# Output projection of a hybrid encoder block: buffers, banks and the order of its pools rearranged

## Chip, core and metric

The kernel runs on one core of a Trainium2 chip. The metric is the device time of one execution in microseconds (us). A difference is called faster or slower from 0.3% on.

## What is computed

One block of a streaming encoder on 2048 tokens of width 1024, in float32. The reference, cut to what matters:

```
xn   = rms_norm(x, norm1_gain);  proj = xn @ w_in
ret  = silu(gate) * head_norm(retention(rotary(q), rotary(k), v))     # 4 heads of 128
rw   = rwkv7_time_mix(proj[..., 2048:], ...)                          # 8 heads of 64, a recurrence in time
h    = x + concat([ret, rw]) @ w_out                                  # the output projection
h    = h + hier_moe(rms_norm(h, norm2_gain), ...)                     # 32 experts, 2 for each token
out  = rms_norm(h, final_norm_gain)
```

## The kernel before

**Two phases with memory of their own.** SBUF and PSUM are given out in pools that are stacked from two ends, "left" (low addresses) and "right" (high addresses), in the order in which they are opened. Within a pool the tiles lie in the order in which the code first takes them, each with its number of buffers. Phase one closes its pools (`rw` left, `ga` right) ahead of the opening of those of phase two, so a tile of phase two lies on bytes or banks of phase one. Its first writer waits until the last reader of each tile that lay there is done (`reuse_waits="tile"`). A planner that runs at build time fixes the order of each engine's instructions and of SyncE's DMA queue: of what is ready in its model it takes the highest priority, and `tc.high_priority(offset=...)` raises one.

**Phase one** walks over four groups of 512 tokens (`g`). The combined projection makes transposed features with matmuls into the two `pj` banks. The RWKV features go through DRAM (`pf_d`) to units of 128 tokens (`u`, 16 of them): `rwkv_prep` loads a unit's features, among them the gate features `lg` (L400, three buffers), and ends with masked products `pt`; a triangular solve runs on GpSimd (L486, L488); `rwkv_inv` completes the inverse on TensorE (from L511 on); `rwkv_chain` carries the state through two chunks; `rwkv_fin` normalizes the rows, multiplies them by the gate that it makes from `lg` with matmuls into `psi` (the line before L579), and writes them to `mx_d` (L580). After the last group's projections the RWKV of the last units is still running. Retention runs once for each head and group in `core`, from the bank `pk`; the last one of all, (g, h) = (3, 3), takes the `pj` banks. It ends with a product of the normalized rows and the head's gate `gs` (L651) and a write to `mx_d` (L652).

**The left side of phase one** opens with the pool `tr`. Its first tile is `lg` (128 columns, 512 bytes a partition, three buffers), then eight buffers of 2048 bytes named `tr`. The left PSUM banks are `pb` (two), `psr`, `psi` and `psz`. The right side opens with `gc` (retention's constants, state and values), then `xp` (x0 to x7), `ntp` (nT0 to nT7), `wh`, `wr`, `ev`, `rk` (kT, qT, gs) and `rc`; its banks are `pj` (two) and `pk`.

**Phase two** first makes the output projection. Its weights are split into a high and a low half (L168, L169) as `wo0` to `wo7`, from raw tiles of two buffers (`mraw`). `tile2(t)` does so with a tile of 128 tokens, whose mixed features are read back from `mx_d` into the same two raw buffers (L737) and split into `mT`. Then 48 matmuls of 512 columns fill two accumulators `acc` (k from 7 down to 0; for each k three matmuls for each half of the columns), and VectorE adds them to the tile's x (L754), which was loaded to `hx` (L742). For tiles 0 to 7 `hx` lies in the pool `hxp` (named `w4`, three buffers), from 8 on in `rwp` (named `raw`, eight buffers). `post(tiles)` routes them: TensorE transposes `hx` with the identity in `ct` (L767), multiplies it by the router's weights, VectorE chooses groups and experts, GpSimd scatters the token numbers, and `hx`, scaled in place (L861), goes to `xt_d` (L862), after which its buffer is free. `ct`, the constant blob of 476 columns, is the first tile of the pool `k2` and is loaded by L698; its first reader is the copy at L710.

The pools of phase two before: left `rwp`, and the banks `tpp` (two) and `accl` (three); right `k2`, `s2`, `mrp`, `wop7`, `wop`, `hxp`, `xhp`, `mtp`, and three `accr` banks. Read with the right side of phase one, `k2` and `s2` lie on `gc` and x7, and `mT` on `rc`.

When all tiles are routed, the expert loop runs: 32 experts, whose weights stream through `rwp` and are split into `hlp`, with accumulators from `accr` and `accl`.

Of the kernel before, what the change touches and what calls it, by code (L numbers as in the profile page):

```python
# [9 lines left out]
F32 = mybir.dt.float32  # L10
F32R = mybir.dt.float32r
# [5 lines left out]
PSUM = bass.MemoryType.PSUM  # L17
# [6 lines left out]
NG = S // G  # L24
# [6 lines left out]
PRI, PRW, PRF, PRC, PRO = 2000, 10000, 9000, 10000, 0  # L31
# [5 lines left out]
NRAW, NSP = 8, ((4, 0, 0), (4, 0, 0), (4, 0, 0))  # L37
# [95 lines left out]
def build(tc, A, out, dbg=None, phases=3):  # L133
    nc = tc.nc
    V, SC, GP, PE, SY = nc.vector, nc.scalar, nc.gpsimd, nc.tensor, nc.sync
# [3 lines left out]
    mx_d = dram.tile([8, 128, S], F32, name="mx_d")  # L139
# [27 lines left out]
    def split_w(hl, raw):  # L167
        SC.copy(hl[:, 0], raw)  # L168
        V.tensor_tensor(hl[:, 1], raw, hl[:, 0].bitcast(F32), op=ALU.subtract)  # L169
# [11 lines left out]
    lp, gp = opener(rw, "left"), opener(ga, "right")  # L181
    tr, rp, sm, cp = lp("tr", 8), lp("rp", 1), lp("sm", 2), lp("cp", 1)
    pb, pr, py, pz = lp("pb", 2, space=PSUM), lp("pr", 1, space=PSUM), lp("py", 1, space=PSUM), lp("pz", 1, space=PSUM)
    gc, xp, ntp = gp("gc", 1), gp("xp", 1), gp("ntp", 1)
    wh, wr, ev, rk, rc = gp("wh", 3), gp("wr", 4), gp("ev", 3), gp("rk", 2), gp("rc", 4)
    pj, pkb = gp("pj", 2, space=PSUM), gp("pk", 1, space=PSUM)
    if True:
        cst = cp.tile([128, CST.shape[1]], F32, name="cst")
        SY.dma_start(cst, A["cst"])
# [421 lines left out]
            mk(f'ret{g}')  # L611

        def core(g, h, kT, qT, gs, vtm):
            pk = pj if (g, h) == (NG - 1, 3) else pkb
            pkn = "pj" if pk is pj else "pk"
            vs = slice((h % 2) * 128, (h % 2 + 1) * 128)
            pst = pk.tile([128, 4, 128], F32, name=pkn)
            for b in range(4):
                PE.transpose(pst[:, b], kT[:, b * 128:(b + 1) * 128], ident)
            ktm = rc.tile([128, 4, 128], F32, name="rc")  # L620
            SC.activation(ktm, pst, AF.Copy, scale=kdec[:, h:h + 1])
            pss = pk.tile([128, 4, 128], F32, name=pkn)
            for b in range(4):
                bs = slice(b * 128, (b + 1) * 128)
                mm(pss[:, b], kT[:, bs], qT[:, bs], b == 0, b == 3)
            sT = rc.tile([128, 4, 128], F32, name="rc")
            V.tensor_tensor(sT, pss, dmask[:, None, h * 128:(h + 1) * 128].to_broadcast([128, 4, 128]), op=ALU.mult)
            psk = pk.tile([128, 4, 128], F32, name=pkn)
            for b in range(4):
                mm(psk[:, b], ktm[:, b], vtm[:, b, vs], b == 0, b == 3)  # L630
            sb = rc.tile([128, 4, 128], F32, name="rc")
            V.tensor_copy(sb[:, 0], srt[:, h])
            for b in range(4):
                dst = sb[:, b + 1] if b < 3 else srt[:, h]
                V.scalar_tensor_tensor(dst, sb[:, b], G128[h], psk[:, b], op0=ALU.mult, op1=ALU.add)
            psy = pk.tile([128, 512], F32, name=pkn)
            for b in range(4):
                bs = slice(b * 128, (b + 1) * 128)
                mm(psy[:, bs], qT[:, bs], sb[:, b], b == 0, b == 3)
            y = rc.tile([128, 512], F32, name="rc")  # L640
            SC.activation(y, psy, AF.Copy, scale=qdec[:, h:h + 1])
            psy = pk.tile([128, 512], F32, name=pkn)
            for b in range(4):
                mm(psy[:, b * 128:(b + 1) * 128], sT[:, b], vtm[:, b, vs], b == 0, b == 3)
            V.tensor_tensor(y, y, psy, op=ALU.add)
            head_center(y, 4, 128, 1e-5, pk.tile([128, 512], F32, name=pkn))
            psn = pk.tile([128, 512], F32, name=pkn)
            for b in range(4):
                PE.transpose(psn[:, b * 128:(b + 1) * 128], y[:, b * 128:(b + 1) * 128], ident)
            mo = rc.tile([128, 512], F32, name="rc")  # L650
            V.scalar_tensor_tensor(mo, psn, hrg[:, h:h + 1], gs, op0=ALU.mult, op1=ALU.mult)  # L651
            SY.dma_start(mx_d[h, :, g * G:(g + 1) * G], mo)  # L652
# [37 lines left out]

    p2, wo_ = ExitStack(), ExitStack()
    lp, kp, gp = opener(p2, "left"), opener(p2, "right"), opener(wo_, "right")
    rwp, tpp, accl = lp("rwp", NRAW), lp("tpp", 2, space=PSUM), lp("accl", 3, space=PSUM)
    k2, s2, accr = kp("k2", 1), kp("s2", 2), kp("accr", 3, space=PSUM)
    mrp, wop7, wop, hxp, xhp, mtp = gp("mrp", 2), gp("wop7", 1), gp("wop", 1), gp("hxp", 3), gp("xhp", 2), gp("mtp", 2)
    if True:
        ct = k2.tile([128, CST2.shape[1]], F32, name="ct")
        SY.dma_start(ct, A["cst2"])  # L698
# [19 lines left out]
            for i in range(4):  # L718
                SY.dma_start(d.rearrange("(i p t) o -> i p (t o)", i=4, p=128)[i], fill[:, z])
        SY.dma_start(h_d[S:S + 128, :], A["x"][0:128, :])  # L720
        wo = [(wop7 if k == 7 else wop).tile([128, 2, 1024], F32R, name=f"wo{k}") for k in range(8)]
        for k in range(7, -1, -1):
            for hf in range(2):
                raw = mrp.tile([128, 512], F32, name="mraw")
                hs = slice(hf * 512, (hf + 1) * 512)
                SY.dma_start(raw, A["wout"][k][:, hs])
                split_w(wo[k][:, :, hs], raw)

        def w4(t):
            return rwp.tile([128, D], F32, name="raw") if t >= PRN else hxp.tile([128, D], F32, name="w4")  # L730
# [1 line left out]
        def tile2(t):  # L732
            r0 = t * 128
            mT = []
            for z in range(1, -1, -1):
                raw = mrp.tile([128, 512], F32, name="mraw").rearrange("p (k t) -> p k t", k=4)
                SY.dma_start(raw, mx_d[z * 4:z * 4 + 4, :, r0:r0 + 128].rearrange("k p t -> p k t"))  # L737
                m = mtp.tile([128, 2, 4, 128], F32R, name="mT")
                split_w(m, raw)
                mT.insert(0, m)  # L740
            hx = w4(t)
            SY.dma_start(hx, A["x"][r0:r0 + 128, :])  # L742
            ps = [accr.tile([128, 512], F32, name="acc") for _ in range(2)]
            for k in range(7, -1, -1):
                ma, mb = (mT[k // 4][:, z, k % 4] for z in range(2))
                for n in range(2):
                    ns = slice(n * 512, (n + 1) * 512)
                    mm(ps[n], ma, wo[k][:, 0, ns], k == 7, False)
                    mm(ps[n], mb, wo[k][:, 0, ns], False, False)
                    mm(ps[n], ma, wo[k][:, 1, ns], False, k == 0)  # L750
            for n in range(2):
                ns = slice(n * 512, (n + 1) * 512)
                with soon():
                    V.tensor_tensor(hx[:, ns], ps[n], hx[:, ns], op=ALU.add)  # L754
            return hx
# [108 lines left out]
        t, PEND = 0, []  # L864
# [20 lines left out]
        gp = opener(p2, "right")  # L885
# [156 lines left out]
        PS, HT, HD = {}, {}, []  # L1042
# [140 lines left out]
        with tc.manual_schedule(engines=MS):  # L1183
            def adds(si):
                while ADD and ADD[0][0] <= si:
                    add_result(*ADD.pop(0)[1:])

            for si, st in enumerate(stages):
                SI[0] = si
                e, w = st  # L1190
                if si:
                    evict(stages[si - 1])
                if si == len(stages) - 4:
                    gfb = k2.tile([128, D], F32, name="gfb", tag="g2b")
                    SC.dma_start(gfb, A["gf"].broadcast_to([128, D]))
                hl = CH.pop(si)
                nps = 2 if w == 2 else 1
                PS[(2 * e, w)] = [accr.tile([128, 512], F32, name="acc") for _ in range(nps)]
                if more(e):
                    PS[(2 * e + 1, w)] = [AL[(na + i) % 3] for i in range(nps)]  # L1200
                    na += nps
                n0, n1, n2 = NSP[w]
                n0 += si < NXS
                splits(min(n0, SB))
                if si:
                    rest(stages[si - 1], HLP)
                HLP = hl
                splits(n0 - min(n0, SB))
                adds(si)
                for half in range(2):  # L1210
                    mms(st, hl, PS[(2 * e, w)], half)
                    if w == 1 and e + 1 < 32:
                        turn(e + 1, half)
                    elif w == 2 and half and more(e + 2):
                        turn1(e + 2)
                    elif HD and (w == 0 or si == len(stages) - 2):
                        hidden_turn(*HD.pop(0))
                    splits(n1 if half == 0 else n2)
                if w == 1 and e + 2 < 32:
                    gather(0, e + 2)  # L1220
            evict(stages[-1])
            rest(stages[-1], HLP)
            adds(len(stages) + 9)
# [52 lines left out]
        for NB in FB:  # L1276
            ss = s2.tile([128, NB], F32, name=f"ssf{NB}")
            HF = []
            for i in range(NB):
                t = t0 + i  # L1280
# [60 lines left out]
```

## Time and profile before

| | us |
|---|---|
| three runs | 2404.76, 2397.96, 2404.65 |
| their median | 2404.65 |
| the profiled execution | 2402.56 |
| its span, first to last instruction | 2400.8 |

A profile tells for each engine when it was busy, and for an instruction that came late what it waited for. PE is TensorE, DVE VectorE, ACT ScalarE, POOL GpSimd and SPq SyncE's DMA queue. PEclk is the share of full speed that TensorE's clock was granted. Times in rows are us from the start of the span unless marked ns. In a row of the timeline, start and duration stand first, then engine, line and operation, output <- inputs, and count; a bracket tells of idle time before it and what ended that. Many instructions have the line of a helper: L152 is each matmul, L168 and L169 are the split, so groups are told apart by their tiles.

### The profile page before, as it was taken

The page shows a single profiled execution, that of the slowest core. Times are in us where ns is not written, and L with a number is a line of the kernel's source. Part 1 is how long each engine was busy: PE and PEld are TensorE (multiplying, and loading weights), DVE is VectorE, ACT ScalarE, POOL GpSimd, SP SyncE. Part 2 cuts the span into 40 slices and gives each one's busy share as a digit, 9 for nine tenths or more (in the row PEclk, how much of TensorE's full clock was granted, in tenths as well). Part 3 has the DMA queues.
Part 4 walks back from the last instruction along what each step waited for, and adds up shares of the span by engine and source line. Part 5 has one row for each costly group of instructions (what it writes and reads, how often), then busy time and mean ns, then how long its engine had stood idle before and what let it go on. Part 6 is the DMA issues. An engine that isn't in the chain of part 4 may idle for free. (4 is left out here: it accounts for less than half of the span.)

```text
span 2400.8 us, 36373 instructions
## 1 busy us (share of the span) xinstructions
PE 2196.5 (91%) x11816; PEld 1803.3 (75%) x11817; DVE 1698.5 (71%) x3594; ACT 1157.2 (48%) x1963; POOL 779.1 (32%) x1405
## 2 busy tenths in 40 slices
PE   5999889998998989999879999599999999999990
PEld 4887678887777877788768888577777777777770
DVE  4477775878766787667775665767777777777775
ACT  4353443434434344343332232267777677776763
POOL 2036444354531575146541433411112111111110
PEclk9999899999999999999969999799999999999995
DMA  6643254433544325433234445289999999999978
GB/s 212 211 148 99 82 172 135 135 94 99 173 142 122 98 88 167 125 101 99 84 96 130 127 163 175 94 304 306 307 321 299 304 300 320 310 293 303 310 233 297
DMA packets 291298, 454.78 MB, mean 189 GB/s; under 512 B 93392, under 2 KB 164496, under 8 KB 291088
## 3 DMA queue, kind: packets, MB, share of 16 engines
q1 hardware_dynamic: 277136, 414.10, 51.7%
q0 software_dynamic: 13824, 37.80, 7.0%
q8 instruction: 94, 1.54, 0.3%
q14 instruction: 100, 0.82, 0.1%
q10 hardware_dynamic: 144, 0.52, 0.1%
HBM read 375.18 MB, written 81.85 MB: 190 GB/s over the span
## 5 line engine op out<-in xcount | busy, mean ns | idle before, releaser
L152 PE MATMUL pj<-nT,whl 128*128 128x512 f32 x2496 | 628.1, 403 | 9.2 <-DVE nT L319 5.2
L152 PEld LDWEIGHTS pj<-nT,whl 128*128 128x128 f32 x2496 | 466.3, 192 | 107.0 <-DVE nT L319 5.7
L914 DVE TENSOR_TENSOR hl<-raw,hl 128x1024 fp32r<-128x1024 f32 x384 | 448.5, 1219 | 121.5 <-ACT hl L913 121.5
L152 PE MATMUL acc<-hl,xT 128*128 128x512 f32 (+1 forms) x2048 | 508.1, 400 | 0.0
L152 PEld LDWEIGHTS acc<-hl,xT 128*128 128x128 f32 (+1 forms) x2048 | 365.0, 182 | 100.0 <-ACT xT L172 0.2
L913 ACT CAST hl<-raw 128x1024 fp32r<-128x1024 f32 x384 | 378.4, 1048 | 6.7 <-PE tp L152 3.0
L249 ACT CAST whl<-wraw 128x512 fp32r<-128x512 f32 x248 | 152.5, 618 | 299.3 <-PE pj L152 236.1
L250 DVE TENSOR_TENSOR whl<-wraw,whl 128x512 fp32r<-128x512 f32 x248 | 188.0, 761 | 144.2 <-ACT whl L249 138.1
L152 PE MATMUL acc<-hl,hT 128*128 128x512 f32 (+1 forms) x1024 | 249.5, 398 | 0.0
L152 PEld LDWEIGHTS acc<-hl,hT 128*128 128x128 f32 (+1 forms) x1024 | 183.1, 181 | 51.8
L486 POOL TENSOR_TENSOR tm<-xl,ln 128x60 f32<-128x60 f32 (+24 forms) x496 | 173.8, 350 | 105.2 <-DMA ln<-nl_d 60.4
L488 POOL TENSOR_TENSOR xl<-xl,tm 128x60 f32<-128x60 f32 (+24 forms) x496 | 195.3, 394 | 36.6
L152 PE MATMUL acc<-wo,mT 128*128 128x512 f32 x768 | 192.3, 402 | 0.0
L1147 POOL DMA_INDIRECT h_d<-yo,ti x48 | 80.1, 1670 | 299.3 <-ACT yo L1139 180.1
L1014 POOL DMA_INDIRECT xb<-xt_d,ti x48 | 49.5, 1031 | 369.6 <-PE tp L1025 288.0
L152 PEld LDWEIGHTS acc<-wo,mT 128*128 128x128 f32 x768 | 142.3, 191 | 28.7 <-DVE mT L169 0.2
L152 PE MATMUL pj<-whl,nT 128*128 128x256 f32 x768 | 114.3, 298 | 0.3 <-DVE gs L600 0.2
L464 DVE TENSOR_TENSOR pt<-pb,cst 64x512 f32<-64x512 f32 x128 | 88.0, 687 | 22.6 <-PE pb L152 20.8
L152 PEld LDWEIGHTS pj<-whl,nT 128*128 128x128 f32 x768 | 101.6, 199 | 3.0 <-DVE gs L600 0.5
L499 POOL COPY mbd<-pt 32x128 f32<-32x128 f32 x64 | 20.7, 323 | 222.9 <-DVE pt L464 199.1
L172 ACT CAST xT<-tp 128x512 fp32r<-128x512 f32 x80 | 47.0, 588 | 82.6 <-PE tp L1025 54.4
L152 PE MATMUL pb<-ar,bk 64*128 64x128 f32 x512 | 76.3, 295 | 5.2 <-DVE pt L464 3.7
(445 smaller groups left out, 3184.5 us busy)
## 6 DMA issues: line engine op xcount, KB each, us to landing
raw<-in_wg_dram SPq DMA_DIRECT2D x128, 512.0 KB
raw<-in_wu_dram SPq DMA_DIRECT2D x128, 512.0 KB
raw<-in_wd_dram SPq DMA_DIRECT2D x128, 512.0 KB
wraw<-in_win_dram SPq DMA_DIRECT2D x208, 256.0 KB
tr<-pf_d SPq DMA_DIRECT2D x80, 256.0 KB
pf_d<-ev SPq DMA_DIRECT2D x52, 256.0 KB
x<-in_xt_dram SPq DMA_DIRECT2D x32, 256.0 KB
pf_d<-x SPq DMA_DIRECT2D x32, 256.0 KB
```

Of the source, the lines that this page charges most:

```text
L152: PE.matmul(o, l, r, start=start, stop=stop)
L172: SC.copy(dst_h, ps)
L249: SC.copy(hl[:, 0], raw)
L250: V.tensor_tensor(hl[:, 1], raw, hl[:, 0].bitcast(F32), op=ALU.subtract)
L464: V.tensor_tensor(pt[zs, i:i + 2, :, z ^ h], psp[h][zs].rearrange("p (f c) x -> p f c x", f=2), maskp[zs, None, None, :].to_broadcast([64, ...
L486: GP.tensor_tensor(tv, xl[:, 0:r, t:t + 1].to_broadcast([128, r, n]), ln[:, t:t + 1, t + 1:32].to_broadcast([128, r, n]), op=ALU.mult)
L488: GP.tensor_tensor(xl[:, 0:r, t + 1:32], xl[:, 0:r, t + 1:32], tv, op=ALU.add)
L499: GP.tensor_copy(mbd[i * 32:(i + 1) * 32, :, i * 32:(i + 1) * 32], pt[i % 2 * 64:i % 2 * 64 + 32, :, i // 2, 0, 32:64])
L913: (SC.copy if hi is SC else hi.tensor_copy)(hl[:, 0], raw)
L914: lo.tensor_tensor(hl[:, 1], raw, hl[:, 0].bitcast(F32), op=ALU.subtract)
L1014: return GP.indirect_dma_start(out=xbs[b], out_offset=None, in_=xt_d, in_offset=bass.IndirectOffsetOnAxis(ap=ti[b][:, e:e + 1], axis=0), b ...
L1147: GP.indirect_dma_start(out=h_d, out_offset=bass.IndirectOffsetOnAxis(ap=idx, axis=0), in_=y, in_offset=None, bounds_check=S + 127, comput ...
```

## The change

- The right side of phase one opens with `xp`, `ntp` and the working pools, and `gc` comes last; of its banks `pk` is opened ahead of `pj`.
- The last retention core uses `pk` as all others do.
- In phase two `k2`, `s2` and `rwp` are opened on the left, in this order. The right side opens with a pool `mxp` (two buffers) for the raw chunks of `mT`, `mrp` (now four buffers, for raw weights alone), `mtp`, and a pool for each weight tile from `wop7` to `wop0`, then `hxp` and `xhp`.
- The right accumulators are two pools: `accs` with one bank, the one of `pk`, and `accr` with the two of `pj`. `acct()` takes every third from `accs`, in the projection and in the expert loop.
- The splits of the weights get the priority of the RWKV chain (PRC), and so do the loads and splits of `mT` of tiles 0 to 2.

```diff
-    gc, xp, ntp = gp("gc", 1), gp("xp", 1), gp("ntp", 1)
-    wh, wr, ev, rk, rc = gp("wh", 3), gp("wr", 4), gp("ev", 3), gp("rk", 2), gp("rc", 4)
-    pj, pkb = gp("pj", 2, space=PSUM), gp("pk", 1, space=PSUM)
+    xp, ntp = gp("xp", 1), gp("ntp", 1)
+    wh, wr, ev, rk, rc, gc = gp("wh", 3), gp("wr", 4), gp("ev", 3), gp("rk", 2), gp("rc", 4), gp("gc", 1)
+    pkb, pj = gp("pk", 1, space=PSUM), gp("pj", 2, space=PSUM)
...
-            pk = pj if (g, h) == (NG - 1, 3) else pkb
-            pkn = "pj" if pk is pj else "pk"
+            pk, pkn = pkb, "pk"
...
-    rwp, tpp, accl = lp("rwp", NRAW), lp("tpp", 2, space=PSUM), lp("accl", 3, space=PSUM)
-    k2, s2, accr = kp("k2", 1), kp("s2", 2), kp("accr", 3, space=PSUM)
-    mrp, wop7, wop, hxp, xhp, mtp = gp("mrp", 2), gp("wop7", 1), gp("wop", 1), gp("hxp", 3), gp("xhp", 2), gp("mtp", 2)
+    k2, s2, rwp = lp("k2", 1), lp("s2", 2), lp("rwp", NRAW)
+    tpp, accl, accs, accr = lp("tpp", 2, space=PSUM), lp("accl", 3, space=PSUM), kp("accs", 1, space=PSUM), kp("accr", 2, space=PSUM)
+    mxp, mrp, mtp = gp("mxp", 2), gp("mrp", 4), gp("mtp", 2)
+    wop = [gp(f"wop{k}", 1) for k in range(7, -1, -1)][::-1]
+    hxp, xhp = gp("hxp", 3), gp("xhp", 2)
...
-        wo = [(wop7 if k == 7 else wop).tile([128, 2, 1024], F32R, name=f"wo{k}") for k in range(8)]
+        wo = [wop[k].tile([128, 2, 1024], F32R, name=f"wo{k}") for k in range(8)]
...
-                split_w(wo[k][:, :, hs], raw)
+                with tc.high_priority(offset=PRC):
+                    split_w(wo[k][:, :, hs], raw)
+
+        NA = [0]
+
+        def acct():
+
+            NA[0] += 1
+            return (accs if NA[0] % 3 == 0 else accr).tile([128, 512], F32, name="acc")
...
-                raw = mrp.tile([128, 512], F32, name="mraw").rearrange("p (k t) -> p k t", k=4)
-                SY.dma_start(raw, mx_d[z * 4:z * 4 + 4, :, r0:r0 + 128].rearrange("k p t -> p k t"))
+                raw = mxp.tile([128, 512], F32, name="mx").rearrange("p (k t) -> p k t", k=4)
                 m = mtp.tile([128, 2, 4, 128], F32R, name="mT")
-                split_w(m, raw)
+                with tc.high_priority(offset=PRC if t < 3 else 0):
+                    SY.dma_start(raw, mx_d[z * 4:z * 4 + 4, :, r0:r0 + 128].rearrange("k p t -> p k t"))
+                    split_w(m, raw)
...
-            ps = [accr.tile([128, 512], F32, name="acc") for _ in range(2)]
+            ps = [acct() for _ in range(2)]
...
-                PS[(2 * e, w)] = [accr.tile([128, 512], F32, name="acc") for _ in range(nps)]
+                PS[(2 * e, w)] = [acct() for _ in range(nps)]
```

## Rows read from the trace of the kernel before

**Rows 1.** The page, busy time of each engine, share of the span, instructions.

```profile
PE 2196.5 (91%) x11816; PEld 1803.3 (75%) x11817; DVE 1698.5 (71%) x3594; ACT 1157.2 (48%) x1963; POOL 779.1 (32%) x1405
```

**Rows 2.** Table of stretches: length, busy PE, PEld, DVE, ACT, POOL, PEclk, DMA, GB/s.

```profile
1187.00:1200.00 13.00, 8.51 (x47) 7.18 (x46) 10.34 (x23) 4.28 (x9) 11.26 (x25) 0.78 0.60 177
1200.00:1260.00 60.00, 42.10 (x234) 37.05 (x233) 45.35 (x125) 21.42 (x47) 28.85 (x70) 0.67 0.34 95
1260.00:1308.50 48.50, 47.91 (x267) 39.87 (x266) 27.12 (x72) 10.97 (x28) 7.91 (x19) 0.97 0.40 116
1308.50:1424.50 116.00, 114.47 (x701) 98.71 (x699) 72.06 (x281) 32.08 (x73) 44.83 (x87) 1.00 0.39 123
1424.50:1530.00 105.50, 104.14 (x582) 89.24 (x580) 68.55 (x326) 31.84 (x77) 42.01 (x42) 0.98 0.56 187
1530.00:1563.00 33.00, 10.01 (x49) 8.62 (x50) 25.43 (x112) 9.30 (x12) 13.14 (x11) 0.53 0.22 69
1563.00:2400.00 837.00, 781.78 (x3638) 605.78 (x3637) 615.90 (x751) 570.47 (x743) 126.93 (x94) 0.97 0.90 301
```

**Rows 3.** Timeline: last write of a retention core, first split of the projection's input.

```profile
1257.21 0.32 SPq L652 DMA_DIRECT2D mx_d<-rc  x1
...
1259.44 1.14 ACT L168 CAST mT<-mraw 128x512 fp32r<-128x512 f32 x2 [1.86 <-DMA mx_d<-rc]
```

**Rows 4.** Groups by line, PE, 1424.5 to 1530: busy us, mean ns.

```profile
L152 PE MATMUL acc<-wo,mT 128*128 128x512 f32 x320 | 80.1, 402 | 0.0
```

**Rows 5.** Timeline of PE: a group of eight matmuls on either side of a pause.

```profile
1157.74 1.00 PE L152 MATMUL psz<-rs__10928,inv 128*128 128x64 f32 x8
...
1194.41 1.97 PE L152 MATMUL psz<-rs__10970,inv 128*128 128x64 f32 x8 [4.49 <-ACT rs__10970 L537]
```

**Rows 6.** Timeline: last core on pj, and the last read of pk.

```profile
1187.97 1.06 PE L152 MATMUL pj<-qT,kT 128*128 128x128 f32 x8
...
1227.60 0.69 ACT L621 ACTIVATE rc<-pj,csg 128x512 f32<-128x512 f32 x1
...
1228.21 0.75 DVE L651 SCALAR_TENSOR_TENSOR rc<-pk,hrg,gs 128x512 f32<-128x512 f32 x1
```

**Rows 7.** The tile lg: duration ns min/median/max, first and last start.

```profile
L152 PE MATMUL psi<-lg,lw x128: 270/275/582, 369.7 to 1423.4; 128*128 128x128 f32 x128
```

**Rows 8.** Timeline: load of ct and its first reader.

```profile
1234.59 0.34 SPq L698 DMA_DIRECT2D ct<-in_cst_dram  x1
...
1240.65 0.17 DVE L710 COPY base<-ct 128x32 f32<-128x32 f32 x1
```

**Rows 9.** The tile ct: the transposes of tiles in hxp, first and last start.

```profile
L767 PE MATMUL tp<-ct,w x48: 270/273/307, 1313.8 to 1401.3; 128*128 128x128 f32 x48
```

**Rows 10.** Timeline of SyncE's queue: unit 15's write, then x loads of tiles 8 on.

```profile
1424.49 0.36 SPq L580 DMA_DIRECT2D mx_d<-yt  x1
1424.90 4.20 SPq L742 DMA_DIRECT2D raw<-in_x_dram  x5
```

**Rows 11.** Timeline: tile 0 is scaled, and the x load that takes its buffer.

```profile
1315.18 1.27 DVE L861 SCALAR_TENSOR_TENSOR w<-w,rs_y,g2b 128x1024 f32<-128x1024 f32 x1
...
1319.96 0.34 SPq L742 DMA_DIRECT2D w<-in_x_dram  x1
```

**Rows 12.** Groups by line, PE, 1260 to 1424.5.

```profile
L152 PE MATMUL acc<-wo,mT 128*128 128x512 f32 x450 | 112.8, 401 | 0.0
```

**Rows 13.** Stretch of PE, instructions on the tile tp alone: length, busy, PEclk, DMA, GB/s.

```profile
1300.00:1424.50 124.50, 21.78 (x174) 1.00 0.37 118
```

**Rows 14.** Timeline of PE: unit 13's inverse to its first use, then unit 15's.

```profile
1208.69 0.30 PE L511 MATMUL psi<-cst,t1s 128*128 128x128 f32 x1 [0.61 <-DMA t1s<-xl_d]
...
1223.42 1.97 PE L152 MATMUL psz<-rs__11287,inv 128*128 128x64 f32 x8
...
1349.03 0.30 PE L511 MATMUL psi<-cst,t1s 128*128 128x128 f32 x1 [1.53 <-DMA t1s<-xl_d]
...
1362.64 1.00 PE L152 MATMUL psz<-rs__11770,inv 128*128 128x64 f32 x8
```

## The prediction

> **What bounds the kernel now.** First the busy shares: TensorE is busy 91% of the span, no other engine comes near [rows 1]. That is an average over stages, so I read next the table of stretches [rows 2]. The experts (1563 us to the end) keep TensorE and the DMA busy throughout; nothing there is edited, so it only slides. From 1260 to 1530 us, where the output projection runs between the last RWKV units and the routing of finished tiles, TensorE is busy 266 of 270 us at a clock of 0.97 to 1.00: every matmul that leaves this stretch or fills a hole before it is worth its own length. From 1187 to 1260 us there are holes: 51 of 73 us busy, clock 0.67 to 0.78. The timeline tells why no projection runs there: the first mT split sits 1.86 us behind the write-out of the last retention core's `rc` tile [rows 3], since mT lies on the bytes of `rc`. From 1530 to 1563 us TensorE waits for the routing of the last tile; that tail keeps its length.
>
> **The start of the projection.** The edit turns the right side around. mT now lies on nT7, x0 and x1, free when the last gemm of the group ends; the weights 7 to 2 lie on nT, whl and wraw; weight 1 lies on ev and on the second gs buffer, the gate of the last head, and weight 0 on kT, qT and gs. The two `accr` banks are now those of pj alone. So tile 0 can run its passes k = 7 to 2 in the holes, 36 of 48 matmuls; k = 1 still waits for the last core's end. A projection matmul costs 80.1 / 320 = 0.250 us [rows 4], so 36 are 9 us and the whole tile 12. With nothing else in the way, that is the gain: 9 to 12 us. The higher priority of the splits and the four raw buffers only serve this; the sixteen loads and splits are the same ones, and they stand ahead of RWKV work on ScalarE and VectorE as before, so I take 0 for them, with 2 us either way: what one or two groups of the chain gain or lose between full and half clock [rows 5].
>
> **The last core on one bank.** Before, its first two results lay in pj and were computed at 1188 us, ahead of the use at 1227.6 us [rows 6]. On pk alone they must wait for the last read of pk by the core ahead, at 1228.2 us, and each later step waits for the eviction of the one ahead: two 8-matmul groups at 1 to 2 us [rows 5] and their evictions, some 6 us. Behind it wait `accs` (second tile), weight 1 and the hxp buffers on `rc`. The Trainium skill, Perfetto Trace Analysis, section Optimizing Tensor Performance, speaks against this edit: independent matmul groups should rotate through different PSUM banks so that evacuation overlaps the next group. By it the early start would shrink from 9 to 3 us; by the step below it is covered anyway.
>
> **The constants of the routing.** This decides. `k2`, `s2` and `rwp` move to the left side, with `k2` first. Pools are stacked from the low end in the order of opening, and a pool's tiles lie in the order of first use. Phase one's left side begins with `tr`, whose first tile is `lg`: three buffers of 512 bytes, 0 to 1535. `k2` begins with `ct`, 476 columns or 1904 bytes. So `ct` lies on all three `lg` buffers, and a tile's load waits for the last reader of what lay there. Each RWKV unit holds its `lg` until its last step, the gate matmul in rwkv_fin; three units are in flight, so unit 15 holds one until 1423.4 us [rows 7]. Before, `ct` lay on the retention constants, was issued at 1234.6 us and was first read at 1240.7 [rows 8], and the routing of tile 0 could transpose with it at 1313.8 us [rows 9]. The trace already shows what the low end of the left side costs: all eight x loads of tiles 8 to 15, whose raw buffers lie there, go out from 1424.90 us on, right behind the write of unit 15 at 1424.49 [rows 10].
>
> `ct` holds the identity of the routing's transposes. Until these have read a tile's hx, the scaled copy can't be made, hx can't be written out, and its hxp buffer isn't free: for tile 0 the scaled copy was made at 1315.18 us, and the x load that took the buffer went out at 1319.96 [rows 11]. hxp has three buffers. So tiles 0 to 2 are evicted, tile 3 and half of tile 4 fill the three accumulators, and then the projection stands until the RWKV is through: 4.5 x 48 = 216 matmuls, where before 450 were done in 1260 to 1424.5 us [rows 12] and 320 were left [rows 4].
>
> The sum at the release, against the profiled execution (2402.56 us, 1.8 above its span, 2.1 below the median):
> - projection: 768 - 216 = 552 left instead of 320, 232 x 0.250 = +58 us. The early tile is already within the 216.
> - routing: TensorE's share of it that was done by then, +21.8 us [rows 13].
> - restart: load of `ct` and first transposes, between 2 and 10 us; the load took at most 6.1 us from issue to first reader [rows 8]. I take +6. In SyncE's queue four more loads for the routing follow `ct`; the plan puts a load where its release is expected, as it did with the eight x loads [rows 10], so I count nothing for others held behind it.
> - after it, tiles 3 to 7 go round in three hxp buffers with no RWKV work as filler: 0 to +15. I take +5, nearer to 0, since the buffer comes back 4.8 us after the transposes' scale [rows 11], against some 12 us of matmuls a tile.
> - the release itself moves. With TensorE empty of projections from about 1326 us (180 matmuls behind 1260 at the pace of [rows 12], 450 in 164.5 us), unit 15 no longer stands behind projection matmuls; but its inverse took 13.6 us beside them and unit 13's took 14.7 without them, at the lower clock [rows 14], so little is gained there. The holes before 1260 us filled may bring some. -30 to +10; I take -8.
>
> Together 58 + 22 + 6 + 5 - 8 = +83 us, about +3.4%: 2404.65 + 83 = 2488 us. VectorE's 69 us in 105 [rows 2] leave it room, so TensorE stays the bound behind the release.
>
> The clock goes with this. Before, behind 4.49 us without a matmul the same 8-matmul group took 1.97 us instead of 1.00 [rows 5], the level of 1.2 instead of 2.4 GHz. TensorE would be in that state while it waits for unit 15, and I have left the release 5 to 10 us later within its bounds for it. The Trainium skill, TensorE: Matmul & The Clock Gate, section HAM oscillation, says that a pause between matmul bursts drops the engine to half rate; the trace agrees with these two rows.
>
> **The rivals.**
> - *The constants don't wait* (the other side). Should `ct` come to lie elsewhere, or `lg` be free before the first transposes would run (1313.8 us is the point from which it decides), the early start pays: 9 to 12 us, less up to 6 for the late last core, 2395 us (2390 to 2402). For it: the holes are real, 22 us of them. Against: the order of opening in the code, and [rows 10].
> - *They wait, but the RWKV tail runs free.* If projection and routing were what slowed units 14 and 15, the release could come 40 us earlier: 83 - 40 = +43, 2447 us. For it: the chain's groups stand between blocks of projection matmuls, 4 to 5 us for 16 to 20 of them by the 0.250. Against: unit 13's inverse without such blocks was no shorter [rows 14], and the clock falls.
> - *No change.* The single bank delays the last core by 6 us, weight 1 and the second tile follow it, and the early tile gives back what it gained: 2403 us. This is where the bank rule above would lead if the constants didn't wait.
>
> **How the numbers follow.** Held constants with the release near its old place 0.74; held with a free tail 0.12; not held, gain 0.10; no change 0.04. The range reaches down over the second case, to 2440, and up to the bounds of the first: release 10 later instead of 8 earlier, restart 10 instead of 6, hxp 15 instead of 5, which is 32 more, 2520. A difference of 0.3%, 7 us, is about what a measurement of this kernel can tell from none. Slower 0.86, same 0.04, faster 0.10.
>
> **What would show it.** Projection matmuls (acc from wo, mT) before 1250 us show the early start, 36 of them or so. The load of `ct` behind the last gate matmul of `lg` shows the held constants; the first transposes that read `ct` follow within 10 us. In between TensorE should be idle for 50 us or more with the clock halved, waiting for projection accumulators whose eviction waits for x. From there to the first expert matmul some 225 us at full clock, and the experts as long as before. If `ct` is loaded before 1320 us, the main step is wrong; if it is loaded at 1380 or earlier behind unit 15, the size of the release is; if TensorE has large holes behind the release, hxp or VectorE was the bound that I put at 5 us.

## The result, and the profile after

The changed kernel takes 2463.4 us (2462.12 to 2469.54, four runs) beside 2401.31 us (2394.65 to 2404.76) for the kernel before on the same chip: ratio 1.0267, 95% interval 1.0236 to 1.0298. It is slower, by 62 us; the forecast was 2488 us, in a range from 2440 to 2520. The profiled execution took 2469.54 us, its span 2467.5.

The table of stretches of after, with the bounds of [rows 2] up to 1530 us (columns as there):

```profile
1187.00:1200.00 13.00, 8.11 (x54) 6.79 (x53) 9.84 (x17) 7.26 (x14) 11.74 (x20) 0.90 0.44 124
1200.00:1260.00 60.00, 46.00 (x258) 39.50 (x257) 38.95 (x105) 19.21 (x42) 22.16 (x45) 0.76 0.35 97
1260.00:1308.50 48.50, 43.39 (x227) 35.37 (x226) 30.82 (x64) 10.44 (x23) 26.77 (x63) 0.91 0.40 108
1308.50:1424.50 116.00, 76.63 (x398) 66.76 (x397) 53.71 (x197) 20.91 (x50) 25.86 (x70) 0.65 0.30 96
1424.50:1530.00 105.50, 105.50 (x570) 90.44 (x569) 51.57 (x208) 29.31 (x65) 29.42 (x30) 0.98 0.42 135
1530.00:1563.00 33.00, 33.00 (x189) 28.55 (x188) 23.06 (x118) 8.35 (x20) 10.97 (x11) 1.00 0.54 168
1563.00:1630.00 67.00, 42.78 (x221) 35.96 (x220) 49.53 (x243) 20.31 (x40) 32.74 (x30) 0.75 0.31 101
1630.00:2467.00 837.00, 781.15 (x3629) 605.07 (x3627) 615.13 (x747) 569.54 (x743) 126.64 (x92) 0.97 0.90 300
```

The last row is the expert stretch: 781.15 us of TensorE in 837, where before had 781.78 in 837 [rows 2]. It only slides. The loss lies ahead of it. From 1308.5 to 1424.5 us TensorE is busy 76.63 us instead of 114.47, at a granted clock of 0.65 instead of 1.00, and then it works without a gap to 1563 on what was left over. The timeline of after's SyncE queue and then of its TensorE shows the cause:

```profile
1368.61 28.27 SPq L580 DMA_DIRECT2D mx_d<-yt  x3
1396.97 0.46 SPq L699 DMA_DIRECT2D ct<-in_cst_dram  x1
...
1399.41 4.80 SPq L752 DMA_DIRECT2D raw<-in_x_dram  x8
...
1414.78 1.62 SPq L752 DMA_DIRECT2D w<-in_x_dram  x2
```

```profile
1328.13 2.77 PE L152 MATMUL acc<-wo,mT 128*128 128x512 f32 x11
...
1399.86 1.97 PE L777 MATMUL tp<-ct,w 128*128 128x128 f32 x8 [4.13 <-DMA ct<-in_cst_dram]
...
1421.72 3.76 PE L152 MATMUL acc<-wo,mT 128*128 128x512 f32 x8
```

`ct` goes out right behind the three last writes of the RWKV rows, at 1396.97 us (before: 1234.59 [rows 8]); the first transposes wait for it until 1399.86; the projection stands from 1330.9 to 1421.72 us, and the x loads that need a free hxp buffer come at 1414.78. The projection's matmuls, grouped by line on TensorE in three stretches (1187 to 1260, 1260 to 1396.5, 1396.5 to 1600):

```profile
L152 PE MATMUL acc<-wo,mT 128*128 128x512 f32 x36 | 13.4, 522 | 4.6 <-DVE mT L169 4.5
L152 PE MATMUL acc<-wo,mT 128*128 128x512 f32 x180 | 44.3, 397 | 0.0
L152 PE MATMUL acc<-wo,mT 128*128 128x512 f32 x552 | 137.9, 404 | 0.0
```

So 36 matmuls run early, 216 are done by the release (the moment at which the last RWKV rows are written and `ct` can go out), and 552 are left.

### The profile page after: what moved, and what is told of

Its sections match the earlier page's. It is cut to its first block, busy times and chain, and to the rows that moved or that the text cites. A ratio compares the mean times of both kernels' runs of the same rounds, so it can differ in the third digit from the quotient of the medians.

```text
span 2467.5 us, 36355 instructions
## 1 busy us (share of the span) xinstructions
PE 2226.7 (90%) x11816; PEld 1829.9 (74%) x11817; DVE 1699.6 (69%) x3594; ACT 1158.4 (47%) x1963; POOL 783.7 (32%) x1405
## 5 line engine op out<-in xcount | busy, mean ns | idle before, releaser
L486 POOL TENSOR_TENSOR tm<-xl,ln 128x60 f32<-128x60 f32 (+24 forms) x496 | 182.1, 367 | 106.7 <-DMA ln<-nl_d 58.0
```

The source lines that it names most:

```text
L486: GP.tensor_tensor(tv, xl[:, 0:r, t:t + 1].to_broadcast([128, r, n]), ln[:, t:t + 1, t + 1:32].to_broadcast([128, r, n]), op=ALU.mult)
```

## The experiments

Each ran in several rounds beside the kernel before on the same chip; a ratio is to that one, with its 95% interval.

### Undoing the parts: who holds the constants

**e2_before_ct_left** is before with `k2` alone put on the left:

```diff
-    rwp, tpp, accl = lp("rwp", NRAW), ...
-    k2, s2, accr = kp("k2", 1), kp("s2", 2), ...
+    k2, rwp, tpp, accl = lp("k2", 1), lp("rwp", NRAW), ...
+    s2, accr = kp("s2", 2), ...
```

> The kernel before with one part of the change alone: k2 opened on the left ahead of rwp, s2 stays on the right. Theory: ct is loaded behind unit 15's last gate matmul; the projection stops at three tiles and a half to four and a half (170 to 216 matmuls), TensorE idles at the lower clock, and the time is 2450 to 2485 us. Rival (the loss is of the other edits): 2400 to 2410 us.

Measured: 2474.09 us, ratio 1.0319 (1.0279 to 1.0358). `ct` goes out at 1399.61 us, behind three writes of `yt` that end at 1399.52. So this one move, without anything else of the change, makes as large a loss and more (73 us by the medians). A part of it can have another cause: without `k2` every right pool slides up, and the first projection matmul comes at 1274.59 us instead of 1260.17.

**e1_lg_behind** is after with `lg` taken behind the first large tiles of `tr`, so that it lies above all of `k2` and `s2`:

```diff
-            lg = tr.tile([128, 128], F32, name="lg", bufs=3)
             kt, sg_, ta, rt, vt = tmp(), tmp(), tmp(), tmp(), tmp()
+            lg = tr.tile([128, 128], F32, name="lg", bufs=3)
```

> The changed kernel, with lg taken behind the eight tr buffers, so that ct lies on tr buffers and no longer on lg; nothing else differs. Theory (the constants are held by unit 15's gate features): ct is loaded when unit 15's preparation ends, 1310 to 1335 us, routing and projection run on beside the RWKV, and the loss goes: 2395 to 2415 us. Rival (the loss comes from the late last core, the single bank and the raised priorities, which all stay): above 2440 us, though ct is early.

Measured: 2464.25 us, ratio 1.0265 (1.0229 to 1.0302), and the queue looks as before the edit:

```profile
1368.07 28.05 SPq L580 DMA_DIRECT2D mx_d<-yt  x3
1396.16 0.50 SPq L699 DMA_DIRECT2D ct<-in_cst_dram  x1
```

This is the miss that matters. `ct` now lies on buffers named `tr` alone, last read in unit 15's preparation; the last instruction of the trace that reads a `tr` tile by that name is its bonus product (`bon`) at 1325.3 us. The load goes out 71 us later, within 0.1 us of the write in front of it in the queue. What holds it is its place in the order of the queue, and no reader of its bytes. Which rule puts it there? `yt`, the rows that `rwkv_fin` writes out, is a tile of the pool `tr` too. So two further kernels move tiles to a pool of their own, opened behind `cp`:

```diff
-    tr, rp, sm, cp = lp("tr", 8), lp("rp", 1), lp("sm", 2), lp("cp", 1)
+    tr, rp, sm, cp, ty = lp("tr", 8), lp("rp", 1), lp("sm", 2), lp("cp", 1), lp("ty", 1)
...
-            lg = tr.tile([128, 128], F32, name="lg", bufs=3)
+            lg = ty.tile([128, 128], F32, name="lg", bufs=3)
...
-                    yt = tr.tile([128, 512], F32, name="yt", bufs=2)
+                    yt = ty.tile([128, 512], F32, name="yt", bufs=2)
```

**e5_lg_yt_out** has all of this, **e6_lg_out** all but the last two lines.

> The kernel after, but lg and yt (the gate features and the result rows) stand in a pool of their own behind cp, so the pool tr on which the constants ct lie holds only tiles that unit 15's preparation is done with. Theory: ct is held in SyncE's order until every tile of the pool tr is released, wherever ct lies in it, so e1_lg_behind changed nothing. Then ct is issued here before 1320 us (after: 1396.97), the projection has 400 to 470 matmuls done when the last mx_d<-yt goes out (after: 216), and the time is 2385 to 2415 us, that is 2463 less the 91 us behind the release, with the tail of unit 15 20 to 30 us slower again. Rival: ct's place in SyncE's order comes from its low priority and not from a pool; then it is issued behind the last mx_d<-yt again and the time is 2455 to 2470.

> As e5_lg_yt_out, but only lg is moved out of tr, yt stays. Theory (the whole pool holds): yt alone holds ct, though no byte of yt lies under it; ct is issued right behind the last mx_d<-yt at about 1397 us, 216 matmuls are done by then, 2455 to 2470 us. Rival (lg is what holds, as a member of the pool): ct before 1320 us and 2385 to 2415 us.

e6 measured 2466.37 us, ratio 1.0285 (1.0262 to 1.0308); e5 2409.77 us, ratio 1.006 (1.0039 to 1.0081). The queue of e6, then that of e5:

```profile
1369.39 28.05 SPq L580 DMA_DIRECT2D mx_d<-yt  x3
1397.50 0.50 SPq L699 DMA_DIRECT2D ct<-in_cst_dram  x1
```

```profile
1317.04 0.51 SPq L699 DMA_DIRECT2D ct<-in_cst_dram  x1
1320.03 0.38 SPq L580 DMA_DIRECT2D mx_d<-yt  x1
1331.33 0.46 SPq L752 DMA_DIRECT2D w<-in_x_dram  x1
...
1425.06 0.38 SPq L580 DMA_DIRECT2D mx_d<-yt  x1
```

With `lg` out and `yt` in, nothing changes, though `yt` lies far above `ct`; with both out `ct` goes out 80 us earlier, the x loads go round, and 450 projection matmuls are done when unit 15 is through, as many as before had [rows 12]. The order of the queue follows the pool: in these three runs `ct` is planned behind the last use of every tile of the pool on whose ground it lies. (`yt` out with `lg` left in wasn't run; that `lg`, whose bytes do lie under `ct` in after, would have held it alone is neither shown nor excluded.) After is 62.1 us over its before by the medians, e5 10.9 over its own (2409.77 against 2398.83); so 51 us of the 62 are this. **e7_before_lg_yt_out** is the control: the same two tiles moved in the kernel before.

> The kernel before with lg and yt in a pool of their own behind cp: what the move of these tiles is worth by itself. There only the raw tiles of tiles 8 to 15 lie over tr, on the left, and their loads went out at 1424.90 us. Theory: these loads are late but not the limit, 2390 to 2408 us, within 0.5% of before; rival: the loads were the limit behind the release, 2375 to 2390 us.

Measured: 2401.77 us, ratio 1.0008 (0.9992 to 1.0024). There the x loads of tiles 8 to 15 begin at 1414.80 instead of 1424.90 us [rows 10], and it is worth nothing: they weren't the limit.

### The constants back on the right

**e4_k2_right** is after with

```diff
-    k2, s2, rwp = lp("k2", 1), lp("s2", 2), lp("rwp", NRAW)
+    rwp, k2, s2 = lp("rwp", NRAW), kp("k2", 1), kp("s2", 2)
```

> The changed kernel with k2 and s2 first on the right, where they lie on x0 to x7, and rwp alone on the left, so that ct can be loaded long before the projection. Theory: as without the overlap, 2395 to 2415 us; the weights 1 and 0 and hxp lie further left, on rc and the retention constants, so the first tile may be some us later. Rival (the other edits cost the time): above 2440 us.

Measured: 2463.18 us, ratio 1.0275 (1.0235 to 1.0315). The constants are early (`ct` goes out at 931.1 us), the loss is the same. Behind the larger `mrp` and `mxp` the right side now reaches down onto tiles of phase one's `cp`, and another load takes the place of `ct` (that its pool places it is argued from the layout; e8 below bears it out):

```profile
1338.85 12.21 SPq L580 DMA_DIRECT2D mx_d<-yt  x2
1351.16 0.45 SPq L717 DMA_DIRECT2D w<-in_spare_dram  x1
...
1366.10 0.37 SPq L580 DMA_DIRECT2D mx_d<-yt  x1
...
1369.96 1.58 SPq L752 DMA_DIRECT2D w<-in_x_dram  x3
```

The fill of the spare rows takes the first hxp buffer (`w`) at 1351.16, and the x loads come at 1369.96; 72 matmuls are done by 1366 us.

**e8_k2_right_small** makes room: `mxp` one buffer and `mrp` two, over the edit of e4.

```diff
-    mxp, mrp, mtp = gp("mxp", 2), gp("mrp", 4), gp("mtp", 2)
+    mxp, mrp, mtp = gp("mxp", 1), gp("mrp", 2), gp("mtp", 2)
```

> The kernel after with k2 and s2 on the right, one buffer for the raw chunks of mT instead of two, and two for raw weights instead of four, so that neither hxp nor xhp lies on the tiles of phase one's cp (in e4_k2_right hxp lay on wbd and xhp on cp's constants). Theory: nothing of phase two but raw waits for unit 15; 350 to 450 matmuls are done before the last mx_d<-yt, and the time is 2390 to 2425 us, a little worse than e5 because one raw buffer lets splits and loads take turns. Rival: the rest of the change (the early start, the order of pj and pk) costs by itself, then it stays over 2430 us.

Measured: 2412.14 us, ratio 1.0072 (1.0049 to 1.0094); 373 matmuls by the release at 1410.4 us. A second way out of the stall, to the same time as e5.

### What the stall costs behind the release

**e3_hxp5** is after with five hxp buffers, so that the projection gets two tiles further before it stands.

```diff
-    hxp, xhp = gp("hxp", 3), gp("xhp", 2)
+    hxp, xhp = gp("hxp", 5), gp("xhp", 2)
```

> The changed kernel with five hxp buffers instead of three: two more tiles, 96 matmuls of 0.25 us or 24 us, before the release. If the tail of the RWKV was quicker because TensorE was empty, the release moves later by about a third of that, 8 us: 2447 us. If the tail's pace has another cause, the release stays at 1396 us: 2439 us. If hxp isn't what stopped the projection at 216 matmuls: 2463 us.

Measured: 2467.65 us, ratio 1.0285 (1.0243 to 1.0326). It did get further: 312 matmuls by 1402 us instead of 216, 24 us of work. Nothing of it arrives at the end: the release comes 4.2 us later (`ct` goes out at 1401.15 us), and the experts start no sooner. The end of the routing on TensorE's timeline, first in after, then in e3:

```profile
1587.62 4.60 PE L152 MATMUL acc<-wo,mT 128*128 128x512 f32 x19
...
1605.37 1.03 PE L152 MATMUL tp<-os,ct 128*128 128x32 f32 x4 [5.03 <-DVE os L835]
...
1626.87 0.79 PE L152 MATMUL acc<-hl,xT 128*128 128x512 f32 x1
```

```profile
1561.04 4.15 PE L152 MATMUL acc<-wo,mT 128*128 128x512 f32 x17
...
1574.24 1.03 PE L152 MATMUL tp<-os,ct 128*128 128x32 f32 x4 [5.32 <-DVE os L835]
...
1597.44 0.61 PE L152 MATMUL tp<-os,ct 128*128 128x32 f32 x2 [8.56 <-DVE os L835]
...
1606.93 1.04 PE L152 MATMUL tp<-os,ct 128*128 128x32 f32 x4 [5.04 <-DVE oh L832]
...
1628.23 0.79 PE L152 MATMUL acc<-hl,xT 128*128 128x512 f32 x1
```

The last projection matmuls end 27 us earlier, the last routing product (`os`) comes 1.6 us later, and the first expert matmul 1.4. From 1565 us on, TensorE in e3 waits for VectorE's steps of the last tiles (5.32, 8.56, 5.04 us). All 16 tiles are routed behind `ct`, and from its load to the last routing product it takes 1605.37 - 1396.97 = 208 us in after, and 206 in e3. Whether another order of the same routing would be shorter wasn't tried.

### What is left: 0.6%

With the stall gone, e5 stays 0.4 to 0.8% over before, about 11 us by the medians. Three parts of the change were undone in e5 one by one. **e9_no_prc** drops the raised priorities:

```diff
-                with tc.high_priority(offset=PRC):
-                    split_w(wo[k][:, :, hs], raw)
+                split_w(wo[k][:, :, hs], raw)
...
-                with tc.high_priority(offset=PRC if t < 3 else 0):
+                with tc.high_priority(offset=0):
```

> e5_lg_yt_out without the raised priority of the weight splits and of the loads and splits of mT of tiles 0 to 2; banks and pools as in e5. e5 is still 11 us over before by the medians. Theory: what is left of the loss is the early start, whose splits run on VectorE and ScalarE ahead of the last retention core and of units 13 and 14; without it the time is 2393 to 2403 us and the last core's write is back near 1257 us. Rival: the rest comes from elsewhere (banks, order of pools), then 2405 to 2415 us.

**e10_one_accr** gives the three right banks back to one pool:

```diff
-    ... kp("accs", 1, space=PSUM), kp("accr", 2, space=PSUM)
+    ... kp("accr", 3, space=PSUM)
...
-            return (accs if NA[0] % 3 == 0 else accr).tile([128, 512], F32, name="acc")
+            return accr.tile([128, 512], F32, name="acc")
```

> e5_lg_yt_out with one pool of three banks in place of accs (one) and accr (two), so the accumulators of projection and expert loop rotate over three banks in their own order. acc's first banks are then pk's, which is free later. Theory (the early start costs, the bank split does nothing in the expert loop): the first projection matmul moves from 1195 us to behind the last core, and the time is 2396 to 2408 us. Rival (the split of the banks slows the expert loop by itself): the span from 1600 us to the end is 5 us or more shorter than in e5, 2393 to 2400 us. If neither, 2405 to 2415 us.

**e11_last_core_pj** gives the last core its pj banks back:

```diff
-            pk, pkn = pkb, "pk"
+            pk = pj if (g, h) == (NG - 1, 3) else pkb
+            pkn = "pj" if pk is pj else "pk"
```

> e5_lg_yt_out with the last retention core on the pj banks, as before. Theory (the wait for pk by the last core is what the rest costs): the last core's write goes from about 1277 us back to 1257 us and the time is 2393 to 2404 us. Rival: the core's end is not on the path that sets the end, since the projection's first six matmul groups don't need its rows sooner than others; 2403 to 2415 us.

Measured: e9 2418.31 us, ratio 1.0068 (1.0055 to 1.0081); e10 2418.22 us, 1.0077 (1.0064 to 1.0091); e11 2411.48 us, 1.0046 (1.003 to 1.0063). None comes back to before, and none is clear of e5's interval. My theories of these three all fell. e9 doesn't take the early start away: 36 matmuls still run early, from 1194.04 us on, and the last core's write comes at 1288.39 us and not near 1257. So it says something of the priorities alone. In e10 and e11 the early start is gone (first projection matmul at 1277.13 and 1280.33 us) and the time stays, so neither the early start, nor the split of the banks (e10), nor the last core's bank (e11) is, one by one, what the rest costs. Their traces do say where the rest lies: the first expert matmul comes at 1576.34 us in e9, 1575.02 in e10 and 1573.06 in e11, 11 to 14 us behind the 1561.89 of before, so it is lost ahead of the expert loop.

**e12_order_alone** is before with the first three lines of the change only: `gc` last, `pk` ahead of `pj`.

> The kernel before with only the first part of the change: on the right side gc is opened last and pk ahead of pj. All of phase two's pools stay as before, so k2 lies on xp and ct loads early, the weight tiles lie on tiles of phase one that come free in another order, and the first accumulator bank is pk's. e5_lg_yt_out, e8, e9, e10 and e11 all stay 0.5 to 0.8% over before, though early start, bank split, the last core's bank and the place of k2 differ among them; this part is common to all of them. Theory: the order of pools and banks of phase one is what the rest costs; then 2410 to 2422 us. Rival: it costs nothing alone, 2396 to 2406 us, and the rest lies in the raw and weight pools of phase two.

Measured: 2431.69 us, ratio 1.0127 (1.0105 to 1.0148): more than the rest that I was looking for. The loads of the raw weights in its queue, and the last core's write:

```profile
1199.52 1.06 SPq L726 DMA_DIRECT2D mraw<-in_wout_dram  x2
...
1262.70 0.33 SPq L652 DMA_DIRECT2D mx_d<-rc  x1
1264.73 0.34 SPq L726 DMA_DIRECT2D mraw<-in_wout_dram  x1
```

After four loads the weights stand for 64 us, until the last core is through; the projection's first matmul comes at 1306 us. Here wo0 to wo6 are one pool, whose low end lies on that core's kT, qT and gs. As far as one trace shows it, that is the rule of the constants from its other side: wo6, high up in the pool, lies by the sizes in the kernel on nT3 to nT5, last read at 1193 us, and yet it is first split at 1263.10 us, behind the core's last read of gs. It is placed by what its whole pool lies on, as `ct` was by the whole pool that lay beneath it. The change's pool for each weight tile takes this wait away, so its parts can't be added up one by one. What the last 0.6% are stays open. The profiled execution of e5, its fastest of four, doesn't hold them: its first expert matmul stands at 1563.00 us, before's at 1561.89.

## Why the prediction was right, step by step

- **What bounds the kernel, and where.** Held: the loss lies between 1260 us and the first expert matmul, and the experts slide.
- **Constants held, 216 matmuls.** The count held to the matmul (36 + 180, then 552), and the stall behind it: projection to transposes to hx to hxp (with two more hxp buffers it was 312 in e3, 96 more). One sign of the stall failed: TensorE should have been idle for 50 us or more. The row below, of after, has 65.6 - 37.7 = 28 us of idle time, since RWKV groups fill the rest, at a mean granted clock of 0.60.

```profile
1330.90:1396.50 65.60, 37.74 (x205) 33.13 (x205) 27.19 (x92) 10.96 (x27) 9.76 (x23) 0.60 0.07 15
```

  The *reason* given for the hold, that `ct` lies on the three `lg` buffers, failed in e1 and e6, where the hold stays without them. The load is planned behind the pool `tr` as a whole, `yt` included. That it gave the right time was luck: the last use of `lg`, at 1395.3 us in after, and the last write of `yt`, done at 1396.9, are the same end of unit 15. A cure drawn from it, to move `lg`, would have been worth nothing.
- **Behind the release.** From the last RWKV write to the end of the last projection matmuls it was 1527.3 - 1424.5 = 102.8 us before and 1592.2 - 1396.5 = 195.7 after: +92.9, where 58 + 22 + 6 + 5 make 91. In before TensorE is busy for all of it; after's two parts are these:

```profile
1396.50:1421.72 25.22, 13.71 (x62) 12.83 (x63) 12.35 (x58) 5.17 (x13) 0.00 (x0) 0.50 0.88 313
1421.72:1592.20 170.48, 170.48 (x920) 145.74 (x918) 97.82 (x457) 46.03 (x107) 58.13 (x58) 0.98 0.43 137
```

  So 11.5 of the 92.9 us are idle, all of it in the restart (put at 6) and none while hxp goes round (put at 5). The other 81.4 are work: the projection's 552 matmuls instead of 320, 137.9 - 80.1 = 57.8 us (put at 58), and the routing with the rest, 23.6 (put at 22). The sum is right, but e3 shows that its terms don't stand apart: with 24 us of projection taken out of it, the routing of all 16 tiles ends no sooner. "TensorE stays the bound behind the release" holds in after to 1592 us, but a second bound stands right behind it: in e3 TensorE has holes from some 1565 us on.
- **The release.** This is the term that was mis-sized: put at -8, it measured 1396.5 - 1424.5 = -28.0 us, from write to write. That is 20 of the 21 us between the +83 of the sum and the 62 measured. (In the profiled pair 92.9 - 28.0 make 65 us, which is how much later the first expert matmul comes; the 62 are by the medians.) Unit 15 in after on TensorE's timeline, from the inverse to its last state product, and that product in before (the first two of before stand in [rows 14]):

```profile
1343.89 0.48 PE L511 MATMUL psi<-cst,t1s 128*128 128x128 f32 x1 [2.05 <-DMA t1s<-xl_d]
...
1354.53 1.97 PE L152 MATMUL psz<-rs__11770,inv 128*128 128x64 f32 x8 [0.66 <-DVE inv L522]
...
1382.49 0.65 PE L152 MATMUL psz<-uv,pt 64*64 64x64 f32 x8 [0.45 <-DVE sbd L552]
```

```profile
1402.33 0.68 PE L152 MATMUL psz<-uv,pt 64*64 64x64 f32 x8
```

The start is 5.1 us earlier, the inverse takes 10.6 us instead of 13.6, the chain 28.0 instead of 39.7, the last unit's rows 14.0 instead of 22.2. And this with groups at half the clock: the eight matmuls at 1354.53 take 1.97 us, those of before 1.00 [rows 14]. So what had stood beside the chain's small groups in before had cost more than the lower clock does. Which part of it isn't shown: projection matmuls, routing and their steps on VectorE and ScalarE all went at once. I had read the inverse alone [rows 14], which shows the least of it. The rival with a free tail put 40 us here; the truth lies between. The runs show the trade as a whole: unit 15 writes its rows at 1366.1 us with 72 projection matmuls done (e4), 1396.5 with 216 (after), 1400.7 with 312 (e3), 1410.4 with 373 (e8) and 1425.1 with 450 (e5). From after to e3 only projection is added, 24 us of it, and unit 15 is 4.2 us later; counted from the first projection matmul (1194.45 and 1188.24 us) it is 10.
- **The early start.** Seen, 36 matmuls, from 1194.5 us on. But the gain of 9 to 12 us didn't come: by 1308.5 us after had 142 projection matmuls done, before 133, that is 2 us. What it cost was put at 0, with 2 us either way. Unit 13's inverse began 13.9 us later than before [rows 14], of which 5.4 us were there when phase one's last gemm ended (1189.6 against 1184.2 us). The timeline of after's TensorE has it:

```profile
1199.42 6.14 PE L152 MATMUL acc<-wo,mT 128*128 128x512 f32 x15 [4.48 <-DVE mT L169]
...
1222.56 0.45 PE L511 MATMUL psi<-cst,t1s 128*128 128x128 f32 x1 [9.41 <-DMA t1s<-xl_d]
```

The early matmuls run at once when their split is there, and the unit's own data come late; whether the one is due to the other no run shows. In e5, where the constants come early, this didn't turn into a gain either.
- **The last core on one bank.** Put at 6 us; its write moved from 1257.21 [rows 3] to 1276.67 us, 19.5 later. e11 shows that the bank isn't the whole reason: with pj back it was at 1279.63 us, later than the 1267.31 of e5, and the early matmuls were gone, so the bank's own price can't be read from it. The rule of the Trainium skill on rotating banks (Perfetto Trace Analysis, section Optimizing Tensor Performance), by which the single bank should have cost most of the early gain, is neither borne out nor refuted by that: e11 and e5 can't be told apart.
- **The rivals.** *The constants don't wait*, built as e5, gave 2410 instead of 2395 us: without the stall this change is no gain, and it lies above the 2403 of *no change* too.

## What to carry to other kernels

Where a planner orders instructions by pools, as here, a tile can inherit the latest end of everything in the pool it lies on, however free its own bytes are (e6), and of what the rest of its own pool lies on (e12); so keep tiles with a late last use in a pool of their own, and look, for each new pool, at the longest-lived tile of the pools beneath. If a load goes out right behind another instruction in its queue, with no gap, suspect the order and not its data. And where a stall empties the bounding engine, what runs beside it gets faster: size that by the whole chain it was slowing, not by its first step.

## What the runs showed of the hardware

TensorE's granted clock fell in both kernels during a pause at the same place of the program, and came back sooner in one than in the other. In before no matmul ran for 3.35 us ahead of 1143.36 us, in after for 5.07 us ahead of 1148.83. Stretches around the pause, before and then after (columns as in [rows 2]):

```profile
1141.00:1142.00 1.00, 0.00 (x0) 0.00 (x0) 0.09 (x1) 0.00 (x0) 0.00 (x0) 1.00 0.31 66
1143.00:1146.00 3.00, 2.64 (x13) 2.67 (x14) 0.29 (x1) 0.00 (x0) 0.00 (x0) 0.50 0.46 81
1147.00:1150.00 3.00, 3.00 (x26) 2.75 (x25) 1.93 (x3) 0.27 (x2) 0.00 (x0) 1.00 0.29 96
```

```profile
1145.00:1146.00 1.00, 0.00 (x0) 0.00 (x0) 0.00 (x0) 0.00 (x0) 0.00 (x0) 1.00 0.14 22
1147.00:1159.00 12.00, 10.17 (x45) 9.72 (x46) 2.51 (x6) 1.82 (x4) 0.00 (x0) 0.50 0.29 75
1160.00:1170.00 10.00, 10.00 (x71) 8.86 (x70) 7.62 (x28) 4.90 (x10) 1.61 (x3) 1.00 0.13 34
```

The clock is at 0.50, the level of 1.2 GHz, from 1143 to 1146 us in before and from 1147 to 1159 us in after. In both TensorE works without a gap from the first matmul behind the pause until the clock is back at 1.00. What makes the second stretch four times as long no run shows. Nor is it shown what it cost: phase one's last gemm ended 5.4 us later in after, but the first matmul behind the pause was already 5.5 us later.
